# A hybrid decoder layer on one core: merge with eleven embedding tiles stored and routing steps spread, experts with splits held back

## Chip, core and metric

The kernel runs on one core of one Trainium2 chip. The metric is the device time of one execution in microseconds (us). Before the change it is 2770.28 us, the median of three runs (2768.61 to 2777.19).

## What is computed

One decoder layer on 2048 tokens of width 1024, all in float32. Cut to what matters here:

```python
u = rmsnorm(h, norm_mix)
q, k, v, c, g = split(u @ w_in)
y_a = diff_attention(q, k, v).reshape(B, S, 512) @ w_attn_out
y_b = silu(layernorm(causal_conv(glu(c)))) @ w_conv_out + b_conv_out
gates = sigmoid(g + b_gate)
h = h + (gates[..., :D] * y_a + gates[..., D:] * y_b) @ w_o      # "merge"
t = rmsnorm(h, norm_ffn)
# 32 experts in 4 groups: best group, its two best experts, blocks of 128 rows per expert
h = h + moe(t)               # hdn = silu(x @ w1[e]) * (x @ w3[e]);  y = hdn @ w2[e]
ple_gate = sigmoid(rmsnorm(h, norm_ple) @ w_ple_gate + b_ple_gate)
h = h + ple_gate * (p @ w_ple_proj)                              # p: 2048 x 256
```

## The kernel before, in words

The engines are called PE (TensorE, matrix products), DVE (VectorE), ACT (ScalarE), POOL (GpSimd) and SP (SyncE, which issues most transfers). Every product is made from float32 operands that are split into a high and a low part: `split` (L91, L92) has ACT write the high part and DVE the low one, and `mm3` (L96 to L98) multiplies high by high, low by high and high by low into one sum. A weight therefore comes in three steps, all in `unit` (L1262): a transfer into `eraw`, a split into `ewh` on ACT, a split into `ewl` on DVE. Tiles come from pools with a fixed number of buffers, so a load waits until an older tile is free.

**Merge** (L650 to L782). Four blocks of 512 tokens, q = 0 to 3. `branch` (L684) loads the attention rows (`braw` from AT, tag "ba") or the convolution rows (from CT, tag "bc"), and splits them; for "ba" PE first turns a scale (`aR`, L694) and DVE applies it. For each of eight column steps j of a block, two sums of four `mm3` (m = 0 attention, m = 1 convolution, tile `mps`) are made, and DVE combines them with the gates `ga` (L743 to L745). Then `wo` (L754 on) multiplies the merged block by w_o, in two halves of four token tiles; each of these eight products is 24 matmuls with 512 columns.

**Routing.** `merge_tail` (L808) is a generator: each `next(routing)` runs one more step. For a block it has `rows_out` (L828: four normed row tiles `tt` stored into T by POOL) and `route` (L838: DVE work that finds each token's two experts, then for each of four token tiles two pairs `oh` and `ob`, L918 and L920, which PE adds into the table `tab`, L924). For the blocks q = 0 to 2 the steps of block q run in block q+1: one after each of the sixteen sums of the column steps, the stores ahead of the route steps, and what is left at once, ahead of `wo`. For q = 3 the steps run at the merge's end; then `pick` (L928) turns the finished table into row indices `idx` (`tabs`, transposed into `tps`, L967; `dps`, L973; `vp`, L981), and POOL gathers the rows of the first experts (`xs`, L1277).

**Embedding.** `projected` (L992) makes one 128-token tile of p @ w_ple_proj: 12 matmuls into two `pps` tiles. `project` (L1003) makes eight of the sixteen at the merge's end and stores them into PJ, one half tile per `next(work)`; the rest is made in the last stage.

**Experts** (`moe`, L1015). A static plan, `SLOTS`, gives each of 32 expert slots its blocks: F is a full block of 128 rows, P a short one of 64. Slots 0 to 9 alternate FF (slot 2: FFP) and P, slots 10 to 13 FP and P, slots 14 to 31 FP and F. The order of all engines is written out by hand: `X` turns a block's rows (`xt`, or `fx` for a short one, one buffer of `fx`), `U` makes the up products (`ups`; f is which half of the width, g which half of the depth), `gated` makes `hd`, `T` turns it into `hh` (`hps`, L1340, then a split on ACT and DVE), `DN` makes the down products (`yd`). A single-block slot leaves its last T and DN in `held`, and the next slot's `release` runs them between its own products. Weight units are put in between by a planner: `did` (L1049) adds an estimated PE time, and as long as the estimated DVE time is behind it, `pull` (L1033) places the next unit's load and splits there. `U` and `DN` pull by force (their first lines) what they need and what is not yet there.

**Last stage** (`ple`, L1370). Sixteen iterations, one per token tile: the two expert rows of each token are loaded (`ys` from Y), added to `h2` (L1412), normed, turned (`tps`, L1292) and multiplied by w_ple_gate (`gps`). `projection` (L1390) either loads a stored tile from PJ or computes it, for the iteration five further on. The order of tiles is 8 to 15, then 0 to 7, so five of the eight tiles that are computed here come ahead of the loop and three in its first three iterations.

Of the kernel before, what the change touches and what calls it, by code (L numbers as in the profile page):

```python
# [9 lines left out]
F32 = mybir.dt.float32  # L10
# [32 lines left out]
MERGE_W = (2, 6)  # L43
AHEAD = 5
EARLY = 4
MOE_W = (8, 14)
# [14 lines left out]
UNIT_US = 1.17  # L61
SLACK = 1.5

PV = {}
# [18 lines left out]
class K:  # L83
# [20 lines left out]
    def build(self):  # L104
        tc, nc = self.tc, self.nc
        with ExitStack() as ctx:
            cp = ctx.enter_context(tc.tile_pool(name="const", bufs=1, reuse_waits="tile"))
            self.dr = ctx.enter_context(tc.tile_pool(name="scratch", bufs=1, space=DRAM, reuse_waits="tile"))
            self.consts(cp)
            dr = self.dr  # L110
            self.QH = dr.tile([H, P, S], F32R, name="QH")
            self.QL = dr.tile([H, P, S], F32R, name="QL")
            self.KH = dr.tile([H, P, S], F32R, name="KH")
            self.KL = dr.tile([H, P, S], F32R, name="KL")
            self.V = dr.tile([H, P, NT, 2, P], F32R, name="V")
            self.G = dr.tile([16, P, S], F32, name="G")
            self.AT = dr.tile([4, P, S], F32, name="AT")
            self.HD = dr.tile([S, D], F32, name="HD")
            self.T = dr.tile([S + PADS, D], F32, name="T")
            self.PJ = dr.tile([S // 2, D], F32, name="PJ")  # L120
            self.Y = dr.tile([2 * (S + PADS), D], F32, name="Y")
            self.ctx = ctx
            self.CT = dr.tile([4, P, S], F32, name="CT")
            with ExitStack() as uctx:
                self.up = uctx.enter_context(tc.tile_pool(name="u", bufs=1, reuse_waits="tile"))
                self.mix()
                self.attn()
            for st in ("keep", "merge", "moe", "ple"):
                if self.stop == st:
                    break  # L130
                getattr(self, st)()
# [520 lines left out]
    def merge(self):  # L652
        tc, nc, A = self.tc, self.nc, self.A
        with ExitStack() as ctx:
# [9 lines left out]
            units = [A["wac"][j] for j in range(NK)] + [wo[a, m, h] for a in range(2) for m in range(2) for h in range(2)]  # L664
            units, ready = units * 4 + halves(A["wpp"]) + halves(A["pT"][0]), []

# [47 lines left out]
            mh, ml = merged()  # L714
            bq = [branch(self.AT, 0, "ba"), branch(self.CT, 0, "bc")]
            for q in range(4):
# [4 lines left out]
                for j in range(NK):  # L721
# [12 lines left out]
                    gate = nc.scalar.activation(ga, ga, AF.Sigmoid)  # L734
                    y = []
                    for m in range(2):
                        ps = pp.tile([P, 512], F32, name="mps", tag="mps")
                        for k in range(4):
                            self.mm3(ps, wh[:, m, k, :], wl[:, m, k, :], br[m][0][:, k, :], br[m][1][:, k, :], k == 0, k == 3)
                        y.append(ps)  # L740
                        if q:
                            next(routing, None)
# [4 lines left out]
                    ga = nga  # L747
                if q:
                    for _ in routing:
                        pass  # L750
                if q < 3:
                    bq = [branch(self.AT, q + 1, "ba"), branch(self.CT, q + 1, "bc")]
                for cc in range(2):
                    w = [tuple(x.rearrange("p (c k j) -> p k c j", c=2, k=2) for x in u) for u in take(4)]  # L754
                    for t in range(4):
# [9 lines left out]
                        self.step()  # L765
                        self.todo.append([LOGITS_AFTER, lambda cc=cc, t=t, hq=hq, lp=lp: self.logits(cc, t, hq, lp)])
                if q == 3:
                    work = self.project(take)
# [5 lines left out]
            for _ in range(3):  # L774
                next(work)
            for steps in (routing, self.pick()):
                for _ in steps:
                    next(work, None)
# [31 lines left out]
    def merge_tail(self, q, hq, ss, lp):  # L810
# [8 lines left out]
        store = self.rows_out(q, hq, r)  # L819
        if q < 3:  # L820
            yield from store
            yield from self.route(q, L)
        else:
            for _ in self.route(q, L):
                next(store, None)
                yield

# [10 lines left out]
    def route(self, q, L):  # L838
# [74 lines left out]
        for t in range(4):  # L913
            made = []
            for k in range(2):
# [5 lines left out]
                made.append((i, oh, ob))  # L921
            yield
            for i, oh, ob in made:
                nc.tensor.matmul(self.tab, oh, ob, start=i == 0, stop=i == 2 * NT - 1)  # L924
# [78 lines left out]
    def project(self, take):  # L1003

        w = take(2)
        for t, tag in zip(range(0, NT // 2, 2), ("bch", "bcl") * 2):
            if t % 4 == 0:
                pt, = take(1)
            o = self.mp.tile([P, 2, D], F32, name="pj", tag=tag)
            for i in range(2):  # L1010
                yield from self.projected(t + i, pt, w, self.pp, "mps", o[:, i, :])
            self.nc.gpsimd.dma_start(self.PJ[t * P : (t + 2) * P, :].rearrange("(i p) d -> p i d", p=P), o)


    def moe(self):  # L1015
# [14 lines left out]

        pe, dve, pulled = 0.0, 0.0, 0

# [16 lines left out]
        def did(us):  # L1049

            nonlocal pe
            pe += us
            while dve <= pe + SLACK and pulled < 12 * NE + 12 and (pulled < MOE_W[1] or pulled - MOE_W[1] in last):
                pull()
# [87 lines left out]
        with tc.manual_schedule(engines=set(self.engines)):  # L1142
# [11 lines left out]
            for i, g in enumerate(groups):  # L1154
                nxt = groups[i + 1] if i + 1 < len(groups) else [None]
                a = g[0]
                for j in g:
                    X(j)
                U(a, 0, 0)
                release()  # L1160
                if len(g) == 2:
                    b = g[1]
# [6 lines left out]
                    U(b, 1, 0)  # L1169
                    T(b, 0)  # L1170
                    U(a, 1, 1)
                    U(b, 1, 1)
                    DN(a, 0, 0)
                    T(a, 1)
                    DN(b, 0, 0)
                    DN(a, 0, 1)
# [7 lines left out]
                else:  # L1184

                    free = lambda j: j is not None and not (a.few and j.few)
                    if free(nxt[0]):
                        X(nxt[0])
                    U(a, 0, 1)
                    release()  # L1190
                    U(a, 1, 0)
                    if not a.few:
                        T(a, 0)
                    if free(nxt[-1]):
                        X(nxt[-1])
                    U(a, 1, 1)
                    if a.few:
                        T(a, 0)
                        held = [lambda a=a: (DN(a, 0, 0), DN(a, 0, 1), T(a, 1)), lambda a=a: (DN(a, 1, 0), DN(a, 1, 1))]
                    else:  # L1200
# [81 lines left out]
    def turned(self, x, few):  # L1282

        nc = self.nc
        n, groups = (FEW, 1) if few else (P, 2)
        into = self.ep.tile([P, NK, 2 * n], F32R, name="xt", tag="fx" if few else "xt", bufs=1 if few else 2)
        each = NK // groups
# [82 lines left out]
    def ple(self):  # L1370
# [7 lines left out]
        self.weights()  # L1378
        order = [*range(8, NT), *range(8)]
        pj, h2, xt = {}, {}, {}  # L1380

        def projection(i):
# [3 lines left out]
            pj[t] = big("pj", "eraw", bufs=self.raws)  # L1386
            if t < 8:
                nc.sync.dma_start(pj[t], self.PJ[t * P : (t + 1) * P, :])
            else:
                for _ in self.projected(t, pt[t % 8 // 4], wpp, self.ed, "ed", pj[t]):  # L1390
                    pass
# [141 lines left out]
```

## Time and profile before

| | |
|---|---|
| median of three runs | 2770.28 us |
| the profiled execution | 2772.82 us |
| its span | 2771.1 us |
| PE busy | 2640.2 us (95%) |
| DVE busy | 1990.0 us (72%) |
| ACT busy | 1454.2 us (52%) |
| mean granted clock of PE | 0.986 |
| moved by transfers | 520.70 MB, 188 GB/s |

The stages by the profile's clock: mixing and attention to 1219 us, merge to about 1693, experts to about 2537, last stage to the end. "Idle before" is time in which an engine ran nothing, and behind the arrow stands what it waited for last. PE's records overlap: a 512-column matmul is recorded as 0.39 us long, while one starts every 0.23 us. So the idle time ahead of a late matmul is shorter than what is lost, which is the distance of the starts less 0.23.

### The profile page before, as it was taken

The numbers are of one execution on the slowest core, as the hardware profiler recorded it, in microseconds if no ns is written. First come the engines' busy times: TensorE is split into PE (matmuls) and PEld (weight loads), VectorE is DVE, ScalarE is ACT, GpSimd is POOL, SyncE is SP. The second block draws the span as 40 slices with busy tenths as digits, with TensorE's granted clock in tenths as the row PEclk, the third lists the DMA queues.
The fourth block names the chain that finished last, engine by engine and source line by source line (L and its number), as shares of the span: only waits on it lengthen the run. The fifth ranks groups of instructions, "written<-read, shape, count | busy, mean of one in ns | idle before, by whom it ended". The sixth has DMA issues, their size and how long they took to land. (4 is left out here: it accounts for less than half of the span.)

```text
span 2771.1 us, 36880 instructions
## 1 busy us (share of the span) xinstructions
PE 2640.2 (95%) x13142; PEld 2162.2 (78%) x13143; DVE 1990.0 (72%) x2974; ACT 1454.2 (52%) x2628; POOL 333.5 (12%) x327
## 2 busy tenths in 40 slices
PE   7999999999999999999999998999999999999998
PEld 5899987898778877877887886767767777776876
DVE  6996237998688888866657546577777777776665
ACT  4232345233666666755444335566766766666542
POOL 2012122022300100000000001111111111210000
PEclk9999999999999999999999998999999999999999
DMA  5133344233624333147646537778888888887462
GB/s 193 65 114 115 125 164 148 76 122 125 197 71 126 94 105 114 49 133 241 221 159 205 203 117 288 248 279 304 294 302 288 305 312 314 279 316 269 138 196 100
DMA packets 181915, 520.70 MB, mean 188 GB/s; under 512 B 19120, under 2 KB 48576, under 8 KB 181216
## 3 DMA queue, kind: packets, MB, share of 16 engines
q1 hardware_dynamic: 139632, 397.02, 43.1%
q0 software_dynamic: 25968, 91.93, 8.8%
q10 hardware_dynamic: 16128, 29.37, 2.8%
q8 instruction: 104, 1.70, 0.2%
q14 instruction: 83, 0.68, 0.1%
HBM read 417.58 MB, written 100.66 MB: 187 GB/s over the span
## 5 line engine op out<-in xcount | busy, mean ns | idle before, releaser
L92 DVE TENSOR_TENSOR ewl<-eraw,ewh 128x1024 fp32r<-128x1024 f32 x464 | 549.6, 1220 | 146.3 <-ACT ewh L91 143.3
L91 ACT ACTIVATE ewh<-eraw 128x1024 fp32r<-128x1024 f32 x464 | 468.3, 1052 | 57.4 <-DMA eraw<-in_wac 17.9
L390 DVE SCALAR_TENSOR_TENSOR co<-cb,pvt,co 128x1024 f32<-128x1024 f32 x240 | 312.7, 1340 | 1.6
L96 PE MATMUL ps<-uh,wh 128*128 128x512 f32 x576 | 232.6, 406 | 4.1 <-ACT uh L91 4.1
L589 DVE TENSOR_REDUCE nm<-sc 128x1 f32<-128x512 f32 (+3 forms) x320 | 185.1, 605 | 63.6 <-PE sc L586 49.4
L97 PE MATMUL ps<-ul,wh 128*128 128x512 f32 x576 | 228.9, 399 | 0.0
L98 PE MATMUL ps<-uh,wl 128*128 128x512 f32 x576 | 227.6, 397 | 0.0
L1315 PE MATMUL ups<-ewh,xt 128*128 128x512 f32 x480 | 194.6, 405 | 5.4 <-ACT ewh L91 5.3
L1316 PE MATMUL ups<-ewl,xt 128*128 128x512 f32 x480 | 189.8, 395 | 2.1 <-DVE ewl L92 2.1
L96 PE MATMUL ps<-wh,uh 128*128 128x384 f32 x512 | 173.2, 338 | 0.0
L98 PE MATMUL ps<-wh,ul 128*128 128x384 f32 x512 | 172.3, 336 | 0.0
L97 PE MATMUL ps<-wl,uh 128*128 128x384 f32 x512 | 172.2, 336 | 0.0
L1253 POOL DMA_INDIRECT Y<-y,dst x49 | 66.1, 1349 | 656.8 <-ACT y L1121 482.3
L96 PEld LDWEIGHTS ps<-uh,wh 128*128 128x128 f32 x576 | 109.2, 190 | 32.1 <-ACT uh L91 4.7
L97 PEld LDWEIGHTS ps<-ul,wh 128*128 128x128 f32 x576 | 109.2, 190 | 28.9 <-issue 1.9
L1318 PE MATMUL ups<-ewh,xt 128*128 128x512 f32 x480 | 130.0, 393 | 0.0
L98 PEld LDWEIGHTS ps<-uh,wl 128*128 128x128 f32 x576 | 108.9, 189 | 26.2
L585 PE MATMUL sc<-Kt,Qt 128*128 128x512 f32 (+2 forms) x320 | 125.8, 399 | 3.0 <-ACT pr L575 2.6
L91 ACT ACTIVATE ah<-tp 128x512 fp32r<-128x512 f32 x144 | 82.4, 602 | 81.6 <-PE tp L635 69.4
L92 DVE TENSOR_TENSOR wl<-wraw,wh 128x1024 fp32r<-128x1024 f32 (+1 forms) x50 | 77.3, 1548 | 64.7 <-ACT wh L91 59.2
L575 ACT ACTIVATE pr<-sc,top 128x512 f32<-128x512 f32 (+3 forms) x176 | 109.1, 631 | 20.2 <-DVE top L596 20.1
L422 ACT COPY qk<-ps 128x256 f32<-128x256 f32 x64 | 23.9, 373 | 179.9 <-PE ps L98 143.4
(338 smaller groups left out, 6763.4 us busy)
## 6 DMA issues: line engine op xcount, KB each, us to landing
eraw<-in_we SPq DMA_DIRECT2D x384, 512.0 KB, 5.4
G<-sg POOLq DMA_DIRECT2D x64, 256.0 KB, 2.9
ga<-G SPq DMA_DIRECT2D x32, 512.0 KB, 5.9
eraw<-in_wac SPq DMA_DIRECT2D x32, 512.0 KB, 4.6
eraw<-in_wo SPq DMA_DIRECT2D x32, 512.0 KB, 4.7
ys<-Y SPq DMA_DIRECT2D x32, 512.0 KB, 7.6
wraw<-in_wqkv SPq DMA_DIRECT2D x16, 768.0 KB, 4.3
wraw<-in_wg SPq DMA_DIRECT2D x20, 512.0 KB, 3.7
```

Of the source, the lines that this page charges most:

```text
L91: nc.scalar.activation(hi, x, AF.Copy)
L92: (lo_eng or nc.vector).tensor_tensor(lo, x, f32(hi), ALU.subtract)
L96: nc.tensor.matmul(ps, lh, rh, start=start, stop=False)
L97: nc.tensor.matmul(ps, lh, rl, start=False, stop=False)
L98: nc.tensor.matmul(ps, ll, rh, start=False, stop=stop)
L390: nc.vector.scalar_tensor_tensor(acc, cb[:, i : i + HALF], wi, acc, ALU.mult, ALU.add)
L575: nc.scalar.activation(pr[c][:, m, : ws[c]], scs[c][:, : ws[c]], AF.Exp, bias=top, accum_out=sums[:, qi, m, c : c + 1])
L585: nc.tensor.matmul(sc[:, :n], Qt[:, 2 * m, qs], ks, start=True, stop=False)
L589: nc.vector.tensor_reduce(nm[:, qi, m, c : c + 1], sc[:, :w], AX.X, ALU.max, negate=True)
L1315: self.nc.tensor.matmul(ps, xt[:, k, :P], wk[0], start=k == 0, stop=False)
L1316: self.nc.tensor.matmul(ps, xt[:, k, :P], wk[1], start=False, stop=False)
L1318: self.nc.tensor.matmul(ps, xt[:, k, P:], wk[0], start=False, stop=k == NK - 1)
```

## The change

Six edits. (1) In the merge's column steps the convolution sum (m = 1) comes first, and for q = 0 the attention branch is only made behind the first convolution sum. (2) Routing is spread: the stores go along with the route steps for all blocks, the blocks q < 3 get one more step ahead of each pair of `tab` matmuls, the `wo` phase takes eight more steps, and what is left is run behind `wo`. (3) Eleven instead of eight embedding tiles are made at the merge's end and stored; there one half tile follows each step of the last block's routing, and steps 3 and 4 of `pick`. The last stage begins with tile 11. (4) `fx` has two buffers, the next block is turned earlier, and a held short block does its second T ahead of its DN. (5) From slot 14 on the planner pulls nothing during U(a,0,0) and the release behind it if something is held, and nothing during U(b,1,1), DN(a,0,0), T(a,1). (6) PJ grows to eleven tiles, and one more half of p is loaded and split at the merge's end.

```diff
+STORED = NT - AHEAD
+LATE = 1 + max(s for s, plan in enumerate(SLOTS) if plan == [PART])
...
-            units, ready = units * 4 + halves(A["wpp"]) + halves(A["pT"][0]), []
+            units, ready = units * 4 + halves(A["wpp"]) + halves(A["pT"][0]) + halves(A["pT"][1])[:1], []
...
-            bq = [branch(self.AT, 0, "ba"), branch(self.CT, 0, "bc")]
+            bq = [None, branch(self.CT, 0, "bc")]
...
-                    y = []
-                    for m in range(2):
+                    y = {}
+                    for m in (1, 0):
+                        if br[m] is None:
+                            br[m] = branch(self.AT, q, "ba")
...
-                if q:
-                    for _ in routing:
-                        pass
                 if q < 3:
                     bq = [branch(self.AT, q + 1, "ba"), branch(self.CT, q + 1, "bc")]
...
+                        if q:
+                            next(routing, None)
+                if q:
+                    for _ in routing:
+                        pass
...
-            for steps in (routing, self.pick()):
-                for _ in steps:
+            for _ in routing:
+                next(work, None)
+            for i, _ in enumerate(self.pick()):
+                if i in (3, 4):
                     next(work, None)
...
-        if q < 3:
-            yield from store
-            yield from self.route(q, L)
-        else:
-            for _ in self.route(q, L):
-                next(store, None)
-                yield
+        for _ in self.route(q, L):
+            next(store, None)
+            yield
...
             yield
+            if q < 3:
+                yield
             for i, oh, ob in made:
...
-        for t, tag in zip(range(0, NT // 2, 2), ("bch", "bcl") * 2):
+        for t, tag in zip(range(0, STORED, 2), ("bch", "bcl", "bah", "bal") * 2):
...
-            while dve <= pe + SLACK and pulled < 12 * NE + 12 and (pulled < MOE_W[1] or pulled - MOE_W[1] in last):
+            while not hold and dve <= pe + SLACK and pulled < 12 * NE + 12 and (pulled < MOE_W[1] or pulled - MOE_W[1] in last):
...
+                hold = bool(held) and a.e >= LATE
                 U(a, 0, 0)
                 release()
+                hold = False
...
                     T(b, 0)
+                    if nxt[0] and nxt[0].few:
+                        X(nxt[0])
                     U(a, 1, 1)
+                    hold = a.e >= LATE
                     U(b, 1, 1)
                     DN(a, 0, 0)
                     T(a, 1)
+                    hold = False
...
-                    free = lambda j: j is not None and not (a.few and j.few)
-                    if free(nxt[0]):
-                        X(nxt[0])
+                    X(nxt[0])
...
-                        held = [lambda a=a: (DN(a, 0, 0), DN(a, 0, 1), T(a, 1)), lambda a=a: (DN(a, 1, 0), DN(a, 1, 1))]
+                        held = [lambda a=a: (T(a, 1), DN(a, 0, 0), DN(a, 0, 1)), lambda a=a: (DN(a, 1, 0), DN(a, 1, 1))]
...
-        into = self.ep.tile([P, NK, 2 * n], F32R, name="xt", tag="fx" if few else "xt", bufs=1 if few else 2)
+        into = self.ep.tile([P, NK, 2 * n], F32R, name="xt", tag="fx" if few else "xt", bufs=2)
...
-        order = [*range(8, NT), *range(8)]
+        order = [*range(STORED, NT), *range(STORED)]
...
-            if t < 8:
+            if t < STORED:
```

Three places show what moves. In the changed file the lines of the helpers lie two further down, those behind them four to nine.

**First**, PE in block q = 1, at the end of the eight column steps and the start of `wo` (`mps` sums, `tab` the routing table, `aR` the scale of the next block). Before:

```order
L97 MATMUL mps<-bcl,ewh 128x512
L98 MATMUL mps<-bch,ewl 128x512
L924 MATMUL tab<-ob,oh 128x512 x2
L694 MATMUL aR<-cst,sub_std 128x128 x8
L96 MATMUL mps<-ewh,mh 128x512
L924 MATMUL tab<-ob,oh 128x512
L97 MATMUL mps<-ewl,mh 128x512
L924 MATMUL tab<-ob,oh 128x512
```

With the change:

```order
L99 MATMUL mps<-bcl,ewh 128x512
L100 MATMUL mps<-bch,ewl 128x512
L930 MATMUL tab<-ob,oh 128x512 x2
L98 MATMUL mps<-bah,ewh 128x512
L99 MATMUL mps<-bal,ewh 128x512
...
L930 MATMUL tab<-ob,oh 128x512 x2
...
L100 MATMUL mps<-ewh,ml 128x512
L930 MATMUL tab<-ob,oh 128x512 x2
L98 MATMUL mps<-ewh,mh 128x512
```

The first two `tab` pairs come while the column steps still run, the third and fourth between the products of `wo`, and the sums in front of them alternate convolution and attention.

**Second**, PE at the merge's end (`pps` embedding, `tps` and `dps` steps of `pick`, then the first expert's rows). Before:

```order
L97 MATMUL pps<-ewl,ewh 128x512
L98 MATMUL pps<-ewh,ewl 128x512
L924 MATMUL tab<-ob,oh 128x512 x2
L981 MATMUL vp<-own,vals 1x32 x3
L924 MATMUL tab<-ob,oh 128x512 x6
L967 MATMUL tps<-cst,tabs 128x128 x4
L973 MATMUL dps<-bd,turned 128x128 x4
L1292 MATMUL tps<-cst,xs 128x128 x16
```

With the change:

```order
L930 MATMUL tab<-ob,oh 128x512 x2
L98 MATMUL pps<-ewh 128x512
L99 MATMUL pps<-ewl,ewh 128x512
...
L930 MATMUL tab<-ob,oh 128x512 x2
...
L930 MATMUL tab<-ob,oh 128x512 x2
...
L930 MATMUL tab<-ob,oh 128x512 x2
...
L973 MATMUL tps<-cst,tabs 128x128 x4
...
L979 MATMUL dps<-bd,turned 128x128 x4
L987 MATMUL vp<-own,vals 1x32 x3
...
L1301 MATMUL tps<-cst,xs 128x128 x16
```

Before, 96 `pps` matmuls stand ahead of all `tab` pairs and nothing behind them; now six stand between one `tab` pair and the next, six behind the last, six behind `tps` and six behind `dps` and `vp`.

**Third**, DVE in a pair of slots of the late experts (`ewl` weight splits, `hd` the gated values, `hh` their turned and split form). Before:

```order
L1332 TENSOR_TENSOR hd<-hd,ups 128x256
L92 TENSOR_TENSOR ewl<-eraw,ewh 128x1024 x6
L92 TENSOR_TENSOR hh<-hps,hh 128x256
L92 TENSOR_TENSOR ewl<-eraw,ewh 128x1024 x3
L1332 TENSOR_TENSOR hd<-hd,ups 128x256
L92 TENSOR_TENSOR ewl<-eraw,ewh 128x1024 x2
```

With the change:

```order
L1341 TENSOR_TENSOR hd<-hd,ups 128x256
L94 TENSOR_TENSOR ewl<-eraw,ewh 128x1024 x4
L94 TENSOR_TENSOR hh<-hps,hh 128x256
L94 TENSOR_TENSOR ewl<-eraw,ewh 128x1024 x4
L1341 TENSOR_TENSOR hd<-hd,ups 128x256
L94 TENSOR_TENSOR ewl<-eraw,ewh 128x1024 x2
```

Two of the six weight splits that stood ahead of `hh` now stand behind it, and one of the following ones goes in elsewhere.

## Rows read from the trace of the kernel before

**Rows 1.** The page: busy time of each engine, its share of the span, instructions.

```profile
PE 2640.2 (95%) x13142; PEld 2162.2 (78%) x13143; DVE 1990.0 (72%) x2974; ACT 1454.2 (52%) x2628; POOL 333.5 (12%) x327
```

**Rows 2.** Late experts' window: length; busy of PE, PEld, DVE, ACT, POOL; clock; DMA, GB/s.

```profile
2045.00:2510.00 465.00, 443.49 (x2038) 338.61 (x2037) 348.87 (x417) 315.60 (x451) 73.05 (x53) 0.99 0.86 301
```

**Rows 3.** PE's waits in blocks q = 1 to 3: us in total, times, longest.

```profile
PE tab L924 <- DVE ob L920: 7.7, 3, 3.0
```

**Rows 4.** PE's timeline at 1378 us: start, length, instruction, idle time before.

```profile
1378.51 0.39 PE L98 MATMUL mps<-bch,ewl 128*128 128x512 f32 x1
1381.15 0.95 PE L924 MATMUL tab<-ob,oh 128*128 128x512 f32 x2 [2.25 <-DVE ob L920]
```

**Rows 5.** DVE's load beside that wait, and behind it: windows, columns as above.

```profile
1380.00:1400.00 20.00, 18.59 (x83) 14.94 (x84) 17.98 (x37) 9.57 (x14) 0.00 (x0) 0.91 0.58 176
1400.00:1420.00 20.00, 20.00 (x108) 17.16 (x107) 8.28 (x10) 9.72 (x17) 0.00 (x0) 1.00 0.52 160
```

**Rows 6.** Windows around three waits of PE and one wait without a slower clock.

```profile
1379.00:1386.00 7.00, 4.85 (x18) 3.83 (x19) 7.00 (x20) 4.01 (x5) 0.00 (x0) 0.76 0.61 193
1797.00:1802.50 5.50, 4.55 (x13) 3.15 (x14) 4.22 (x5) 3.00 (x4) 0.00 (x0) 0.69 0.87 273
2101.00:2107.00 6.00, 5.35 (x16) 3.69 (x16) 3.61 (x5) 3.14 (x6) 0.00 (x0) 0.72 0.78 271
2131.00:2136.00 5.00, 4.28 (x19) 3.45 (x19) 3.16 (x4) 2.87 (x4) 0.57 (x1) 1.00 0.96 362
```

**Rows 7.** PE's timeline at the merge's end.

```profile
1676.86 0.62 PE L924 MATMUL tab<-ob,oh 128*128 128x512 f32 x2
...
1693.17 1.09 PE L1292 MATMUL tps<-cst,xs 128*128 128x128 f32 x4 [7.21 <-DMA xs<-T,idx]
```

**Rows 8.** The chain that ended last, last stage: start, length, piece.

```profile
2590.90 0.87 PE tps L1292 x8
2605.41 0.87 PE tps L1292 x8
2617.19 0.87 PE tps L1292 x8
...
2673.49 8.98 DMA ys<-Y
```

**Rows 9.** PE's waits in the experts' stage, 1700 to 2090 us.

```profile
PE ups L1300 <- DVE xt L92: 5.4, 3, 3.3
...
PE yd L1300 <- DVE hh L92: 3.3, 4, 1.1
PE hps L1340 <- DVE xt L92: 3.2, 4, 1.2
```

**Rows 10.** PE's waits in the experts' stage, 2095 to 2515 us.

```profile
PE yd L98 <- DVE hh L92: 11.5, 17, 0.7
PE yd L96 <- ACT hh L91: 3.5, 3, 1.2
```

**Rows 11.** DVE's timeline ahead of one such wait.

```profile
2277.84 6.90 DVE L92 TENSOR_TENSOR ewl<-eraw,ewh 128x1024 fp32r<-128x1024 f32 x6 [0.53 <-ACT ewh L91]
2284.66 0.42 DVE L92 TENSOR_TENSOR hh<-hps,hh 128x256 fp32r<-128x256 f32 x1
```

**Rows 12.** PE's timeline: the same late matmul in two pairs of slots.

```profile
2285.13 0.50 PE L98 MATMUL yd<-ewh,hh 128*128 128x512 f32 x1 [0.72 <-DVE hh L92]
...
2335.46 0.50 PE L98 MATMUL yd<-ewh,hh 128*128 128x512 f32 x1 [0.72 <-DVE hh L92]
```

**Rows 13.** PE's timeline where a weight came late.

```profile
2070.24 0.49 PE L1315 MATMUL ups<-ewh,xt 128*128 128x512 f32 x1 [1.81 <-ACT ewh L91]
2071.50 0.50 PE L1316 MATMUL ups<-ewl,xt 128*128 128x512 f32 x1 [0.77 <-DVE ewl L92]
```

**Rows 14.** PE's waits at the merge's start, 1200 to 1295 us.

```profile
PE aR L694 <- DVE sub_std L682: 3.3, 1, 3.3
...
PE mps L96 <- ACT ewh L91: 2.6, 1, 2.6
```

More of the change, by code (lines that the diff above doesn't have):

```diff
@@ L119, in build @@
             self.T = dr.tile([S + PADS, D], F32, name="T")
-            self.PJ = dr.tile([S // 2, D], F32, name="PJ")
+            self.PJ = dr.tile([STORED * P, D], F32, name="PJ")
             self.Y = dr.tile([2 * (S + PADS), D], F32, name="Y")
@@ L739, in merge @@
                             self.mm3(ps, wh[:, m, k, :], wl[:, m, k, :], br[m][0][:, k, :], br[m][1][:, k, :], k == 0, k == 3)
-                        y.append(ps)
+                        y[m] = ps
                         if q:
@@ L1009, in project @@
             o = self.mp.tile([P, 2, D], F32, name="pj", tag=tag)
-            for i in range(2):
+            n = min(2, STORED - t)
+            for i in range(n):
                 yield from self.projected(t + i, pt, w, self.pp, "mps", o[:, i, :])
-            self.nc.gpsimd.dma_start(self.PJ[t * P : (t + 2) * P, :].rearrange("(i p) d -> p i d", p=P), o)
+            self.nc.gpsimd.dma_start(self.PJ[t * P : (t + n) * P, :].rearrange("(i p) d -> p i d", p=P), o[:, :n, :])
     def moe(self):
@@ L1029, in moe @@
         self.last = W
-        pe, dve, pulled = 0.0, 0.0, 0
+        pe, dve, pulled, hold = 0.0, 0.0, 0, False
         def pull():
@@ L1193, in moe @@
                         T(a, 0)
-                    if free(nxt[-1]):
-                        X(nxt[-1])
+                    X(nxt[-1])
                     U(a, 1, 1)
```

## Prediction

> **What bounds the kernel now.** I read the page first: PE is busy for 95% of the span, DVE for 72%, ACT for 52% [rows 1]. So only time in which PE stands still, or runs at a slower clock, can be won, some 130 us of 2771 by the difference. A window over the late experts then shows whether another engine could take over: the transfers' share is 0.86 and DVE is busy 348.87 of 465 us, so neither is full [rows 2]. Last I read, stage by stage, which wait ends last before PE goes on. There are four kinds: PE waits for `ob` ahead of the routing table [rows 3]; for the chain from the table to the gathered rows at the merge's end [rows 7]; for `xt` and `hh` among the early experts [rows 9]; and for `hh` among the late ones [rows 10]. In front of each DVE has the awaited piece behind other work.
>
> A wait costs more than its idle time, in two ways. The start of the late matmul lies 2.64 us behind the start before it, where 0.23 is normal: 2.41 lost for 2.25 recorded [rows 4], so I add 0.17 per wait. And the granted clock falls behind some: 0.76 over 7 us, 0.69 over 5.5 us and 0.72 over 6 us, against 1.00 around a wait of 0.72 us [rows 6]. Its two levels are 1.2 and 2.4 GHz, so these are 7 × 0.24/0.5 = 3.4 us at the lower one, and 3.4 and 3.4 likewise; matmuls that run there take twice as long, so each such stretch costs about 1.7 us.
>
> **The change, part by part**, against the profiled execution's 2772.8 us, which is 2.5 above the median of the runs.
>
> *Routing spread.* Three waits for `ob` are 7.7 us [rows 3]; with 3 × 0.17 and a slow stretch behind each (1.7 × 3) they cost 13.3. DVE is busy 17.98 of 20 us there, and only 8.28 of the 20 us behind it, in `wo` [rows 5]. Two of four `tab` pairs move into `wo`, and the pairs left have a step more between making `ob` and using it. DVE's work only moves to where it has 11 idle us in 20. The two pairs left in the column steps can still meet the same backlog. I take 11 off; the ends are 4 (one wait of three goes) and 13.3. The row stores stay four per block on POOL, beside the same route steps, and cost nothing: none of their tiles is awaited here. What they could delay next is the w_o weights' splits on DVE, and the lighter `wo` phase covers that.
>
> *Three more tiles at the merge's end.* Each tile is 12 matmuls. In the last stage one goes from each of the first three iterations; the third of these is 14.51 us long (2590.90 to 2605.41), the next one, without a tile, 11.78 [rows 8], so a tile is 2.73 us of PE and three are 8.2. But further on the chain goes through the loads of `ys`, 8.98 us each, which wait for buffers and for DVE [rows 8]; a loop that comes there 8 us sooner waits there longer. I let 1.6 go: 6.6 won. At the merge's end PE starts the first `tab` at 1676.86 and the first expert's turn at 1693.17, with 7.21 us of that idle in one piece [rows 7]. The 36 moved matmuls fit into that idle time, but six of them, 1.36 us, stand now between one `tab` pair and the next, and six ahead of each of `tps` and `dps`, where PE waited for DVE before. An estimate from 1.36 less the short waits that they fill: 0.4 later for each of the three gaps, 0.5 for each of the two steps behind, 2.2 in all for `idx` and the gather. On ACT the split of the extra half of p stands ahead of the copies and of what the routing starts from; one split there can put all later by up to 2, and I take 1.4. POOL issues a sixth PJ store ahead of the gather; its last product stands six matmuls behind `dps`, about as long as DVE needs to make `idx` from `dps`, so I count no wait. Together 3 off (6.6 less 3.6); ends 2 lost and 9 won.
>
> *Early experts.* PE waits 5.4 us in three pieces for `xt` of a single-buffered or late-turned block [rows 9], one of them with a slow clock behind it [rows 6]: 5.4 + 0.5 + 1.7 = 7.6. The second `fx` and the earlier X take these away, since the turn then has a whole up phase to be split. The waits on `hh` at L1300 (3.3 in four) shrink by about 1, as T(a,1) now comes two down products sooner. The waits of `hps` for `xt` (3.2) [rows 9] are a turn that stands right ahead of T and holds both its PSUM buffers; one or two more turns come into that place, 2.6 given back. Net 6 off; ends 0 and 9. The gathers go out as early as their turns, on a POOL queue in which Y stores stand behind them; no row shows one awaited there.
>
> *Late experts.* Seventeen waits on DVE's `hh` are 11.5 us and three on ACT's 3.5 [rows 10]; with 20 × 0.17 and one slow stretch [rows 6] this is 20.1. The cause is in DVE's timeline: six weight splits, 6.90 us, run ahead of the `hh` that PE needs [rows 11]. Two of them moved behind it are 2.3 us, more than the longest of these DVE waits, 0.7, so all of them should go. The price: splits that are held come later to the `U` that needs them. By the planner's own order the splits are then 0 to 3 ahead of their use from slot 14 to 18 where they were 3 to 7, and from slot 21 on 7 or more as before. A weight that comes late is seen once: 1.81 for `ewh`, 0.77 for `ewl` behind it [rows 13], with 2 × 0.17 and a slow stretch 4.6. I take one such and 1.4 of small ones: 14 off; ends 20 won, and a loss that is a rival below.
>
> *Merge's start.* The two waits there, 3.3 and 2.6 us [rows 14], end with the scale's input and with the first weight. The first weight's load stands on SP behind a load that waits for a buffer, in both orders; with convolution first PE has less to wait for ahead of it, and more behind. I take 0, between 3 won and 3 lost.
>
> Sum: 11 + 3 + 6 + 14 = 34 off, 2772.8 − 34 = 2738.8; less the 2.5 by which that execution was long, **2736.3 us**.
>
> **The rivals.**
>
> *Half of it* (chance 0.17). The splits put off run ahead of the next `hh` or `ob` in place of the last. For it: over a pair DVE's load is unchanged, and 17.98 of 20 us is close to full [rows 5]. Against: DVE has gaps in the late stage [rows 2]. Half of 11 and of 14 are lost: 2736.3 + 12.5 = 2749.
>
> *The late waits are for buffers* (0.04). Then the pause of 0.7 us, the same at each slot, ends when a PSUM or SBUF tile comes free; postponed splits don't change it, and the hold's price stays: 2736.3 + 14 + 6 = 2756. Against it: the row names `hh`, and DVE starts that `hh` right at the end of the sixth split [rows 11], so the awaited thing is data. The Trainium skill, Perfetto Trace Analysis, section Optimization Strategy, has this reading: the same gap that repeats on the engine that should be full can mean too few buffers for the next tile. By it the term of the late experts would be nothing; by the row it is 14.
>
> *The hold starves PE of weights*, slower (0.06). From slot 14 each of nine pairs has its splits, 24 in a pair, put off during two stretches, and the lead never comes back; each pair then shows one late weight. The dearest row is that for slot 14 with 4.6 us; one with two tries would be 6 to 7. Break-even: the other terms win 20, the waits taken away 20.1; 40/9 = 4.5 us per pair. At 6.5 the sum is 9 × 6.5 = 58 lost, 2770.3 − 40 + 58 = 2788. It decides where DVE's time outside the held stretches is less than its splits need: a pair takes 50.33 us (2285.13 to 2335.46) [rows 12], DVE is busy 348.87 / 465 of it [rows 2], 37.8 us, and the held stretches are about 7.4 us (32 matmuls at 0.23). Of its 12.5 idle us at least 5 are then left: near, but enough. A milder form, 4 us per pair, gives 2766, no change (0.06).
>
> *The merge's end is later by all it could win* (0.11): the routing starts 2 us later on ACT's account and the last stage wins nothing past the `ys` loads: −5 in place of +3, 2744.
>
> *All of it* (0.08): the upper ends, 13.3 + 9 + 9 + 20 = 51: 2719.
>
> **How the numbers follow.** The forecast itself has 0.48. The range runs from 2721 to 2756: it leaves out both forms of the starved PE (0.12) and the half of the full gain that lies lower, 0.16 in all. About 0.3%, 8.3 us, is what a measurement can tell from no change. Faster by more than that are all cases but the two starved ones: 0.88; within it the milder one, 0.06; slower the other, 0.06.
>
> **What would show it.** Right: no wait of `tab` on `ob` above 1 us in q = 1 to 3 and a clock of 1.00 there; the first three iterations of the last stage near 11.8 us; no wait on `hh` in the late experts, and a pair in less than 49 us where it was 50.3 [rows 12]; the transfers' share still below 0.9. Wrong: new waits of `ups` on `ewh` or `ewl` (L1315 and L1316 before) behind slot 14, a gathered row (`xs`) later than 16 us behind the first `tab`, or waits that only change their name. The forecast falls if the late experts win less than 8 us.

## The result, and the profile after

The changed kernel takes 2756.85 us (median of five runs, 2754.28 to 2761.91), before 2770.28: a ratio of 0.9948, interval 0.9935 to 0.9961. It is faster, by 13.4 us where 34 were forecast, and the time lies 0.85 us above the range's upper end. The profiled execution's span is 2755.1 us (before 2771.1), so its own parts have to explain 16.0.

Five starts in PE's timeline and the end of the span cut both executions into the same stages:

| from, to | before | after | difference | forecast |
|---|---|---|---|---|
| start, last matmul of attention | 1218.66 | 1219.55 | +0.9 | 0 |
| to the first column sum of q = 1 | 113.84 | 119.84 | +6.0 | 0 |
| to the first `pps` | 319.17 | 312.42 | −6.8 | −11 |
| to the first `ups` | 45.61 | 47.41 | +1.8 | +3.6 |
| to the first `gps` | 859.31 | 849.06 | −10.3 | −20 |
| to the end | 214.51 | 206.82 | −7.7 | −6.6 |

The page's first part and the window over the late experts, for [rows 1] and [rows 2]: PE is busy 8.6 us less, but over a shorter span, and does more in the 465 us.

```profile
PE 2631.6 (96%) x13142; PEld 2160.4 (78%) x13143; DVE 1993.0 (72%) x2975; ACT 1453.7 (53%) x2629; POOL 331.3 (12%) x329
```

```profile
2045.00:2510.00 465.00, 454.50 (x2094) 348.90 (x2093) 358.76 (x426) 323.24 (x464) 69.37 (x53) 0.99 0.87 306
```

Two stages are far off the forecast: the first block of the merge, and the experts. PE's waits, in the same columns as before (us in total, times, longest), show where. From 1200 to 1295 us, the window of [rows 14], one row of the kernel before that [rows 14] leaves out, and two with the change:

```profile
PE mps L97 <- DVE ewl L92: 2.7, 1, 2.7
```

```profile
PE aR L696 <- DVE braw L697: 6.0, 1, 6.0
PE mps L98 <- ACT ewh L93: 5.4, 1, 5.4
```

The 5.4 stands ahead of the first column sum and costs nothing: that sum starts 10.2 us behind attention, where it was 11.0. The 2.7, a w_o weight that comes late, and the 6.0 both stand at the other end of block q = 0, at the start of its w_o. With the change the clock fell there too; the windows below (columns as in [rows 2]) are of the kernel before and of the changed one:

```profile
1283.00:1290.00 7.00, 5.33 (x23) 4.22 (x24) 5.55 (x8) 5.22 (x7) 0.00 (x0) 1.00 0.84 264
```

```profile
1283.00:1290.00 7.00, 3.94 (x15) 3.36 (x16) 6.00 (x9) 4.48 (x7) 0.00 (x0) 0.53 0.59 173
```

In blocks q = 1 to 3, for [rows 3], the three waits of `tab` for `ob` are gone, and two other ones stand there:

```profile
PE aR L696 <- DVE braw L697: 3.9, 2, 2.0
PE pre L894 <- DVE r L889: 1.4, 3, 0.6
```

Among the early experts, for [rows 9], no `xt` is waited for at L1309 (L1300 before), but `tps`, the turn of a block, waits seven times for `hh`:

```profile
PE tps L1301 <- DVE hh L94: 7.8, 7, 2.6
...
PE hps L1349 <- DVE xt L94: 4.7, 4, 1.9
...
PE yd L1309 <- DVE hh L94: 2.1, 3, 1.1
```

And among the late ones, for [rows 10], the waits of 11.5 and 3.5 us have become 3.0, with two kinds of late weights beside it:

```profile
PE yd L1312 <- DVE hh L94: 3.0, 4, 0.8
PE ups L1325 <- DVE ewl L94: 1.7, 2, 1.1
PE ups L1324 <- ACT ewh L93: 0.6, 1, 0.6
```

At the merge's end, for [rows 7], the gathered rows are turned 18.92 us behind the first `tab`, where it was 16.31, with three more tiles made by then:

```profile
1676.30 0.62 PE L930 MATMUL tab<-ob,oh 128*128 128x512 f32 x2
...
1695.22 1.09 PE L1301 MATMUL tps<-cst,xs 128*128 128x128 f32 x4 [6.49 <-DMA xs<-T,idx]
```

And the chain of the last stage, for [rows 8], now goes through loads of `ys` from early on, one every 12.6 to 13.6 us:

```profile
2580.24 8.32 DMA ys<-Y
...
2593.25 7.98 DMA ys<-Y
```

One of the seven new waits of `tps` among the early experts, on PE and then on DVE (start, length, instruction, idle before):

```profile
2037.99 0.38 PE L1349 MATMUL hps<-cst,hd 128*128 128x128 f32 x2
...
2040.16 0.33 PE L1349 MATMUL hps<-cst,hd 64*128 64x64 f32 x2
2042.11 0.71 PE L1301 MATMUL tps<-cst,xs 64*128 64x64 f32 x8 [1.61 <-DVE hh L94]
```

```profile
2039.35 2.36 DVE L94 TENSOR_TENSOR ewl<-eraw,ewh 128x1024 fp32r<-128x1024 f32 x2 [0.53 <-ACT ewh L93]
2041.63 0.42 DVE L94 TENSOR_TENSOR hh<-hps,hh 128x256 fp32r<-128x256 f32 x1
2041.97 1.22 DVE L94 TENSOR_TENSOR ewl<-eraw,ewh 128x1024 fp32r<-128x1024 f32 x1
2043.10 0.28 DVE L94 TENSOR_TENSOR hh<-hps,hh 128x128 fp32r<-128x128 f32 x1
```

The turn (`tps`) comes right behind two turns of `hd` (`hps`). All three use PSUM tiles of one pool with two buffers, so `tps` starts when DVE has read the first `hps` (2042.05, `tps` at 2042.11); and DVE has two weight splits ahead of that `hh`. Six of the seven waits, 7.3 of the 7.8 us, are of such a short block's turn.

### The profile page after: what moved, and what is told of

The parts are those of the page before. It is cut to its first block, busy times and chain, and to the rows that moved or that the text cites. A ratio compares the mean times of both kernels' runs of the same rounds, so it can differ in the third digit from the quotient of the medians.

```text
span 2755.1 us, 36909 instructions
## 1 busy us (share of the span) xinstructions
PE 2631.6 (96%) x13142; PEld 2160.4 (78%) x13143; DVE 1993.0 (72%) x2975; ACT 1453.7 (53%) x2629; POOL 331.3 (12%) x329
```

## The experiments

Each run changes only what its diff shows. Times are medians; the intervals are of the ratio to the kernel before, run on the same chip.

**Edit 1 taken back.** Both branches ahead of the loop, attention first.

```diff
-            bq = [None, branch(self.CT, 0, "bc")]
+            bq = [branch(self.AT, 0, "ba"), branch(self.CT, 0, "bc")]
...
-                    for m in (1, 0):
+                    for m in (0, 1):
```

> Edit 1 taken back alone: both branches are made ahead of the column steps and the attention sum comes first again; all else as changed. Theory: the 6.0 us wait of aR for DVE's braw in block q = 0 comes from edit 1, because the next block's first two scales no longer run ahead of the column steps; the 1.9 and 2.0 us waits of aR in q = 1 and 2 come from the spread routing, which takes the table matmuls away from in front of them, and stay. Then 6 to 7 us less than the changed kernel's 2756.9: 2750 to 2751, with two aR waits of about 2 us left. Rival: the attention sum as the last of each column step frees its tiles late in all blocks; then all three waits go, 10 to 11 us, 2746. Second rival: nothing is won, since the merge's start is bound by the first loads: 2756 to 2757.

2751.22 us, 0.9919 [0.9896, 0.9941]. From the last attention matmul to q = 1 it takes 111.9 us, where the changed kernel took 119.8. Its waits, at the merge's start and in q = 1 to 3:

```profile
PE aR L696 <- DVE sub_std L684: 3.3, 1, 3.3
PE mps L98 <- ACT ewh L93: 2.0, 1, 2.0
PE mps L99 <- DVE ewl L94: 1.5, 1, 1.5
...
PE aR L696 <- DVE braw L697: 0.4, 1, 0.4
```

```profile
PE aR L696 <- DVE braw L697: 3.2, 2, 2.0
```

The wait of 6.0 us is gone, the two of about 2 us are not. Edit 1 costs some 6 us, in block q = 0: in the profiled executions of all versions that have it, this stretch takes 118.1 to 120.4 us, in those of all without it 111.9 to 115.9. The other waits belong to the spread routing.

**Convolution first in q = 0 alone.**

```diff
-                    for m in (1, 0):
+                    for m in (0, 1) if q else (1, 0):
```

> As changed, but the convolution sum comes first only in block q = 0; in q = 1 to 3 the attention sum is first again. Theory (edit 1 costs in q = 0, the other two waits belong to the spread routing): no change, 2755 to 2758, all three aR waits remain (6.0, 1.9, 2.0). Rival (tiles freed late): the waits of 1.9 and 2.0 go, about 4 us less, 2753.

2758.28 us, 0.9958 [0.9942, 0.9975]: no change against 0.9948. The `aR` waits are 4.8 at the start and 3.2 in two later. The order of the sums in q = 1 to 3 is innocent. No run separates the order in q = 0 from the late attention branch; the traces speak for the branch. Before, DVE scaled the next block's first two tiles within the column steps of q = 0 (at 1252 and 1254 us); with edit 1 all four come behind them, the first at 1285.26, and DVE has first to split a weight of w_o whose high part it waits 2.26 us for.

**The next branches behind the first product of w_o.**

```diff
-                if q < 3:
-                    bq = [branch(self.AT, q + 1, "ba"), branch(self.CT, q + 1, "bc")]
...
+                        if q < 3 and cc == 0 and t == 0:
+                            bq = [branch(self.AT, q + 1, "ba"), branch(self.CT, q + 1, "bc")]
```

> As changed, but the next block's branches are written behind the first product of w_o instead of ahead of it. Theory: PE's waits of 6.0, 1.9 and 2.0 us for aR are DVE being behind with the column steps' work and a late weight; with one product of 5.5 us ahead of it the aR waits shrink to under 1 us each, a wait of about 2.7 for the w_o weight stays in q = 0: 6 to 8 us less, 2749 to 2751. Rival: the wait is for the loads of the next block's rows, which start when their buffers are free, and only moves along: 2756 to 2758.

2762.00 us (2754.79 to 2762.86), 0.9954 [0.9940, 0.9968]: nothing won. With `aR` out of the way (0.2 us are left) PE waits at the same place for the last column's `mh` (1.3, and 2.9 in two later) and for the weights of w_o (0.9 for the high part and 0.8 for the low one; the 5.0 in the first row stands at the merge's start):

```profile
PE mps L98 <- ACT ewh L93: 5.9, 2, 5.0
...
PE mps L98 <- ACT mh L93: 1.3, 1, 1.3
PE mps L99 <- DVE ewl L94: 0.8, 1, 0.8
```

```profile
PE mps L98 <- ACT mh L93: 2.9, 2, 1.7
```

The border between column steps and w_o has several late inputs at once; taking one away shows the next. The `aR` waits shrank as this run's theory said, but its gain did not come; the rival's time came, but PE waits there for other things than the rows that the rival named.

**The next short block turned one up product later.**

```diff
-                    if nxt[0] and nxt[0].few:
-                        X(nxt[0])
                     U(a, 1, 1)
+                    if nxt[0] and nxt[0].few:
+                        X(nxt[0])
```

> As changed, but in a pair of blocks the next short block is turned behind U(a,1,1) instead of ahead of it. Theory: the seven waits of that turn (tps) for hh, 7.8 us, come from the two PSUM buffers of T and X: both are held by the turns of hd made right ahead of it until DVE has split them. One up product (2.7 us) later they are free: the waits go, with the slow-clock stretches behind the longest (two of 1.7): 8 to 11 us less, 2746 to 2749. Rival: DVE is the bound among the early experts, and the wait only moves to the next turn (hps) or to hh of the down products: under 3 us won, 2754 to 2757.

2742.97 us, 0.9887 [0.9861, 0.9913]: 14 us less than the changed kernel by the medians, more than expected. The waits from 1700 to 2055 us:

```profile
PE hps L1349 <- DVE xt L94: 3.8, 4, 1.2
...
PE yd L1309 <- DVE hh L94: 2.7, 4, 1.2
...
PE tps L1301 <- DVE hh L94: 0.5, 1, 0.5
```

Of seven `tps` waits one is left, 0.5 us, the only one of a full block's turn, which this edit does not move; all six of the short blocks' turn are gone. From the first `ups` to the first `gps` it takes 836.7 us, 12.4 less than the changed kernel; the rest of the 14 is not in this stage.

**Edit 4 taken back.** The change's lines for the experts without the holds, turned round; in short:

```diff
-                    if nxt[0] and nxt[0].few:
-                        X(nxt[0])
                     U(a, 1, 1)
...
-                    X(nxt[0])
+                    free = lambda j: j is not None and not (a.few and j.few)
+                    if free(nxt[0]):
+                        X(nxt[0])
...
-                        held = [lambda a=a: (T(a, 1), DN(a, 0, 0), DN(a, 0, 1)), lambda a=a: (DN(a, 1, 0), DN(a, 1, 1))]
+                        held = [lambda a=a: (DN(a, 0, 0), DN(a, 0, 1), T(a, 1)), lambda a=a: (DN(a, 1, 0), DN(a, 1, 1))]
...
-        into = self.ep.tile([P, NK, 2 * n], F32R, name="xt", tag="fx" if few else "xt", bufs=2)
+        into = self.ep.tile([P, NK, 2 * n], F32R, name="xt", tag="fx" if few else "xt", bufs=1 if few else 2)
```

> Edit 4 taken back alone: one fx buffer, X and the held T and DN where they were; the hold from slot 14, the merge and the embedding as changed. Theory: edit 4 only exchanged waits for xt (5.4 us) for waits of the turn for hh (7.8 us); taking it back gives 1 to 4 us, 2753 to 2756, with the tps waits gone and the three xt waits back. Rival: edit 4 won the 6 us that were forecast and the loss lies elsewhere: 2762 to 2764.

2752.07 us, 0.9921 [0.9901, 0.9941]. The `tps` waits for `hh` are gone and the three `xt` waits are back. The same stage takes 844.7 us: the hold alone won 859.3 − 844.7 = 14.7, edit 4 as made lost 849.1 − 844.7 = 4.4, and with the turn one step later it wins 844.7 − 836.7 = 8.0. These are single executions; the five versions that have the changed kernel's expert code took 847.5 to 851.9 us, so the loss is small but clear of that spread.

**The hold off.**

```diff
-LATE = 1 + max(s for s, plan in enumerate(SLOTS) if plan == [PART])
+LATE = 99
```

> As changed, but the hold from slot 14 never applies. Theory: the hold is worth what was forecast for it, 12 to 15 us; without it the waits of the down products for hh come back, 0.6 and 0.7 us twice in each pair of slots, and the late weights behind slot 16 (0.6 and 1.1 us) go: 2769 to 2772. Rival: the gain of the late stage comes from edit 4 (earlier turns) or from a shorter chain, not from the hold: 2757 to 2762.

2773.08 us, 0.9998 [0.9988, 1.0008], about 1 us more than expected. The stage takes 865.6 us, so with edit 4 in place the hold is worth 16.5; and without the hold edit 4 loses 865.6 − 859.3 = 6.3. The late weights behind slot 14 are gone, and from 2060 to 2515 us the waits of [rows 10] are back:

```profile
PE yd L100 <- DVE hh L94: 10.9, 16, 0.7
PE yd L98 <- ACT hh L93: 3.5, 3, 1.2
```

**Eight tiles stored.**

```diff
-STORED = NT - AHEAD
+STORED = 8
```

With eight, the extra half of p is not loaded at the merge's end either.

> As changed, but only eight embedding tiles are stored, as before; the table's pairs still get half tiles between them as long as there are some. Theory: three more tiles at the merge's end cost about 2 us there and win 7 to 8 in the last stage: 2761 to 2764. Rival: the loads of ys bound the last stage, and the three tiles are worth under 2 us: 2756 to 2759.

2765.69 us, 0.9972 [0.9959, 0.9985]: the three tiles are worth 6.6 us by the ratios (0.0024 × 2770). The last stage takes 216.3 us, where every version with eleven tiles took 205.1 to 207.6.

**Both mends together**: the first diff above and that of the turn one product later.

> Both mends together: edit 1 taken back, and the next short block turned one up product later. Theory: they lie in different stages and add up: 5.6 and 13.9 us off 2756.9, 2736 to 2739, close to the forecast's 2736.3. Rival: an earlier merge only shifts the start of the experts into a later weight, and part is lost: 2742 or more.

2734.91 us, 0.9865 [0.9848, 0.9881]. The two mends add up: 21.9 us won together, 5.6 and 13.9 alone.

**The spread taken back in that version**: stores first, no extra step, the rest ahead of w_o.

```diff
+                if q:
+                    for _ in routing:
+                        pass
                 if q < 3:
                     bq = [branch(self.AT, q + 1, "ba"), branch(self.CT, q + 1, "bc")]
...
-                        if q:
-                            next(routing, None)
-                if q:
-                    for _ in routing:
-                        pass
...
+        if q < 3:
+            yield from store
+            yield from self.route(q, L)
+        else:
+            for _ in self.route(q, L):
+                next(store, None)
+                yield
...
-            if q < 3:
-                yield
```

> The version with both mends (order undone, turn later; 2734.9 us), and the spread of the routing taken back for blocks q = 0 to 2: stores ahead, no extra step, the rest at once ahead of w_o. Theory: the three waits of tab for ob come back with their slow-clock stretches (13 us), the aR waits of 2.5 and 1.3 us go, as PE stands at tab in front of them: 8 to 10 us more, 2743 to 2745. Rival: the spread wins all 11 that were forecast or more and the aR waits are from elsewhere: 2746 or more with aR waits still there.

2743.88 us, 0.9890 [0.9873, 0.9906]: 9.0 us more. From 1295 to 1640 us:

```profile
PE tab L930 <- DVE ob L926: 8.9, 4, 3.0
```

No `aR` wait is left: the spread takes these waits away and pays part of it back as `aR`. From the first column sum of q = 1 to the first `pps` it takes 318.6 us (before 319.2), where the twelve versions with the spread took 310.4 to 316.7, so the stage shows some 6 us, less than the medians' 9. The merge itself varies: from its first column sum to the first `pps` five executions with the same merge code (edit 1 taken back, spread kept) took 412 to 420 us.

**Only the second hold**, in the version with both mends.

```diff
-                hold = bool(held) and a.e >= LATE
+                hold = False
```

> The version with both mends, and only the second hold (behind U(a,1,1) in a pair); nothing is held during U(a,0,0) and the release. Theory: each hold takes away one of the two waits of a pair: without the first the eight waits of 0.72 us ahead of the down products of the single block come back, 0.9 each with the start: 6 to 8 us more, 2741 to 2743. Rival: one hold is enough, since its splits only move to another place: 2734 to 2737.

2736.43 us, 0.9868 [0.9851, 0.9884]: the rival's time, and yet not for the rival's reason. Waits from 2060 to 2500 us, of this run and then of the version with both holds:

```profile
PE yd L100 <- DVE hh L94: 6.0, 9, 0.7
PE yd L1312 <- DVE hh L94: 1.5, 2, 0.8
```

```profile
PE yd L1312 <- DVE hh L94: 3.0, 4, 0.8
PE ups L1325 <- DVE ewl L94: 1.7, 2, 1.1
PE ups L1324 <- ACT ewh L93: 0.6, 1, 0.6
```

Without the first hold its waits of 0.7 do come back, nine of them, but the late weights are gone. One turn of a short block to the next is one pair; in the version with both holds first, then without the first one:

```profile
2350.10 0.71 PE L1301 MATMUL tps<-cst,xs 64*128 64x64 f32 x8
...
2398.40 0.71 PE L1301 MATMUL tps<-cst,xs 64*128 64x64 f32 x8
```

```profile
2347.20 0.71 PE L1301 MATMUL tps<-cst,xs 64*128 64x64 f32 x8
...
2396.49 0.71 PE L1301 MATMUL tps<-cst,xs 64*128 64x64 f32 x8
```

Late in the stage a pair lasts 48.30 against 49.29 us. The first hold wins 1.0 per pair there, from the turn for slot 24 on, and pays it back in the first pairs, where by the planner's order few splits lie ahead: from the turn for slot 14 to that for slot 18 it takes 107.4 us with it and 103.8 without.

**The hold from slot 18.**

```diff
+LATE = 18
```

> The version with both mends, with the hold from slot 18 on instead of 14. Theory: the weights that came late behind slots 14 and 16 (0.6, 1.15 and 0.6 us, with a slow stretch) are the price of the hold while few splits lie ahead; from slot 18 that price goes, 3 to 4 us, but two pairs get their waits for hh back, 4 to 5 us: 2735 to 2737. Rival: the late weights have nothing to do with the hold: 2739 to 2740.

2734.99 us, 0.9861 [0.9845, 0.9878], as expected: from 2060 us on no weight is late (the one of 1.9 us in slot 14 itself stands in every version), and the early pairs keep their waits for `hh`, 3.3 on ACT and 2.3 on DVE.

**The first hold from slot 16, the second from 14.**

```diff
-                hold = bool(held) and a.e >= LATE
+                hold = bool(held) and a.e >= 16
```

> The version with both mends, and the first hold (U(a,0,0) and the release) only from slot 16 on; the second from 14 as changed. In the run without the first hold the weights of slots 14 and 16 were in time, and each pair lasted 49.3 us with one wait of 0.72; with it, from the sixth pair on, 48.3 without a wait. Theory: the first hold's price is paid once, in slot 14, where few splits lie ahead; left out there, its eight later uses win 1.0 us each against the version without it: 2727 to 2730, no late weight behind slot 14. Rival: the hold costs lead wherever it starts, so the late weights come two slots later, and nothing is won against 2734.9: 2733 to 2737.

2731.29 us, 0.9841 [0.9823, 0.9860], the fastest of all, 1.3 above the expected range; its interval overlaps that of both mends, 0.9848 to 0.9881. In the traces the experts' stage is clearer: 827.2 us from the first `ups` to the first `gps`, against 834.6 with the hold from 14, and no late weight behind slot 14. The turns for slots 16 and 18, with the hold from 14 and then with the first hold from 16:

```profile
2100.25 0.71 PE L1301 MATMUL tps<-cst,xs 64*128 64x64 f32 x8
...
2153.47 0.71 PE L1301 MATMUL tps<-cst,xs 64*128 64x64 f32 x8
```

```profile
2105.96 0.71 PE L1301 MATMUL tps<-cst,xs 64*128 64x64 f32 x8
...
2155.30 0.71 PE L1301 MATMUL tps<-cst,xs 64*128 64x64 f32 x8
```

That pair lasts 49.34 us in place of 53.22, the largest part of the 7.4. Against the version without the first hold it wins 1.0 in this pair, nothing in the next (49.36 against 49.31), and 1.0 in each of the five from slot 20 to 28: of the eight wins that were expected six are seen, and the last pair has no next turn to measure it by.

## Why the prediction was right or wrong

*Late experts, 14 forecast: right*, 14.7. The named cause, six splits ahead of `hh`, is shown by the hold that moves two of them, and by the run without it. Not all waits went, as I had said they would: four, 3.0 us, stayed. The price was there too, the late weights forecast for slots 14 to 18, and the last run shows that one use of the first hold, in slot 14, brought it.

*Three more tiles, 3 forecast*: right in kind, too small. The merge's end cost 1.8 instead of 3.6. From the first `tab` to the gathered rows it took 2.6 longer (2.2 forecast), but the 1.4 for ACT did not come: the first `tab` stands 24.5 us behind the first `pps`, with the extra half of p and in the run without it, and 25.2 before. The last stage gave 7.7 of 8.2. So the `ys` loads, though on the chain, took back less than I gave them.

*Routing, 11 forecast: too large*, by 2 to 5 us. The three waits went as named. In their place came `aR` at the start of w_o, 3.9 us, which nothing in the prediction named. The step that failed is "DVE's work only moves to where it has 11 idle us in 20". I took the first window of [rows 5] for the column steps, but w_o starts in it, at 1382.84: in the first 17 us of w_o DVE was already nearly full, and only what follows has the idle time. So it is with the change, where w_o starts at 1387.87 (first its start before, then the changed kernel's window):

```profile
1382.84 0.78 PE L96 MATMUL mps<-ewh,mh 128*128 128x512 f32 x1
```

```profile
1385.00:1405.00 20.00, 18.11 (x83) 14.70 (x82) 17.74 (x28) 11.16 (x17) 0.00 (x0) 0.91 0.79 254
```

What is late next there is the next block's scale, and, as the run with later branches shows, behind it the last column's own `mh`.

*Early experts, 6 forecast: wrong in sign*, 4.4 lost. The step that failed is "one or two more turns come into that place, 2.6 given back". I had the mechanism, a turn that finds both PSUM buffers held, and its row, but counted it for `hps` behind a turn only. In six pairs of blocks, not one or two, the moved turn itself stood right behind two `hps`: 7.8 us of `tps` waits in place of the 5.4 for `xt`, and the `hps` waits for `xt` grew from 3.2 to 4.7. The rest of the term held: the `xt` waits went, and those at L1300 shrank by 1.2. The step was one product short; moved by it, the term is the 8 of the upper part of its range.

*Merge's start, 0 forecast, at most 3 lost: wrong*, 6.0. The step that failed is "The two waits there": it looked at the waits ahead of the first sums only, where nothing was lost, and left out the third of that window, 2.7 us for a late w_o weight. By the traces, making the attention branch late also takes the next block's first scales out of the column steps, and they queue on DVE behind that weight at the end of the block, 60 us on: 6.0 us of waiting in place of 2.7, and a clock of 0.53 where it was 1.00. That taking edit 1 back wins this is shown; the share of the branch alone is not.

Those two steps were 10.4 and 6.0 us off, 16.4 of the 20.6 between forecast and result. By the stages the routing adds 4.2 and the time ahead of the merge 0.9; the tiles and the late experts take 3.6 back; and 2.5 is what I took off for the long execution before, while the one after lies on its median. (The 0.17 per wait is 0.16 by its own row, which changes nothing.) With both steps mended the time is 2734.91, for a forecast of 2736.3. That it is so close is in part luck: in that version the experts win 24.8 us where 20 were forecast, and the merge from q = 1 on 7.6 where 11 were.

No rival told this. The second comes nearest by its time, 2756, but by it the hold wins nothing, and it won 14.7. The first, 2749, was to bring the waits back on `ob` and `hh`; those on `ob` went, and of those on `hh` 3.0 us stayed. The starved PE did not come. The repeated gap of the late experts was no lack of buffers: the hold, which adds none, takes most of it away. Among the early experts the change itself made such a gap: six short turns wait for one of two PSUM buffers. No run gave them a third buffer.

Of the signs, no wait of `tab` for `ob`, the iterations of the last stage (11.8 us), the pair under 49 us (48.3, from the sixth on) and the transfers' share (0.87) came as named. The clock of 1.00 in q = 1 to 3 did not everywhere: it is 0.91 in the window shown with the routing. Two of the signs of being wrong came as well: new waits of `ups` for weights behind slot 14, and waits that only change their name, `xt` to `tps`. The sign of 16 us behind the first `tab` was badly set, since the kernel before already took 16.31.

The Trainium skill's reading of such gaps (Perfetto Trace Analysis, Optimization Strategy: they can mean too few buffers for the next tile) thus does not fit the late waits, 0.7 us each, and fits the early ones, 7.3 us in six, which I did not look at with it.

## What to carry to other kernels

When work is moved earlier, ask which buffer it needs at its new place and who still holds it; the dependency on its data is the smaller half. Read the same border in all repetitions: an edit at the first block's start showed its price at that block's end. And a rule that postpones work is paid out of the lead at hand, so start it where the lead has grown: the first hold costs 3.5 us over its first two pairs when it starts in slot 14, and wins 1.0 in its first pair when it starts in slot 16.

## What the runs showed of the hardware

Whether PE's clock falls behind a wait does not follow from the wait's length alone. In windows (length; busy of PE, PEld, DVE, ACT, POOL; clock; DMA share, GB/s) around a wait of 1.61 us, at 2042 us, and one of 2.61, at 1721 us, of the changed kernel:

```profile
1716.00:1726.00 10.00, 7.39 (x39) 5.92 (x38) 8.48 (x10) 7.27 (x10) 0.93 (x1) 1.00 1.03 410
2040.00:2050.00 10.00, 8.39 (x36) 6.32 (x36) 5.78 (x9) 4.99 (x9) 0.90 (x1) 0.83 0.63 214
```

The longer one left the clock at its upper level, 2.4 GHz; behind the shorter one 10 × 0.17/0.5 = 3.4 us ran at the lower of the two, 1.2 GHz. My price of a wait, 1.7 us for a slow stretch, is thus certain only where the trace has the stretch.
